# Samples' attention in two steps of four tiles instead of four of two, with a fifth place for cached tiles

## The chip, the core and the metric

The kernel runs on one core of a Trainium2 chip. A core has five engines with a queue of their own each, worked through in order: TensorE (PE in the profile; PEld is its weight load) for matrix products, VectorE (DVE), ScalarE (ACT), GpSimd (POOL) and SyncE (SP), which here issues transfers between the memory outside the core (HBM) and the on-chip memory SBUF. TensorE writes to PSUM, from where VectorE and ScalarE copy results. An engine that needs another's result waits at a semaphore, and all that stands behind that instruction in its queue waits too.

The metric is the device time of one execution in microseconds (us), lower is better. Three runs of the kernel before give 1091.49, 1091.80 and 1091.83 us, median 1091.8.

## The reference

One layer of a decoder for two groups that share all weights: a prompt of 512 tokens and 8 samples of 8 tokens. The layer has three blocks, each with a residual: a mixer (Mamba heads and mLSTM heads), an attention over a memory, and a feed-forward network. The change is in the second block. Cut to what matters:

```python
qx = (u @ w_xq).reshape(bsz, length, X_HEADS, X_HEAD_DIM)          # 4 heads of 256
sc = jnp.einsum('blhd,bmhd->bhlm', qx, mem_k) * (X_HEAD_DIM ** -0.5)
pr = jax.nn.softmax(sc, axis=-1)
o = jnp.einsum('bhlm,bmhd->blhd', pr, mem_v).reshape(bsz, length, X_WIDTH) @ w_xo
x = x + _rms(o) * g_post_x
```

For the prompt, keys and values of the memory (256 entries) are computed here from `w_mem_k` and `w_mem_v`. For the samples they come from a cache, `cache_mem_k` and `cache_mem_v`, with 256 entries and 4 heads of 256 for each of the 8 samples: 8 MB of keys and 8 MB of values in 32-bit floats, which are read once.

## The kernel before

Prompt and samples are 576 columns of the same matrices (512 and 64), so that each weight is loaded once for both. Weights are multiplied in two parts: each 128x1024 tile of weights is loaded by SyncE into one of two buffers `raw` (line 175), ScalarE rounds it to `whi` (L180), VectorE and POOL subtract for the rest `wlo` (L187), and TensorE takes three products, whi with the high part of the activations (L202), whi with their low part (L203), wlo with the high part (L205). There are three buffers of `whi` and `wlo`, so a cast waits until TensorE is through with the tile three before, and a load waits until the split of the tile two before is done.

The attention runs over the four heads of the prompt from 3 down to 0. For each head TensorE computes the queries (`xq`, tiles ps_xq), the memory's keys (`mem_key`, ps_mk, 48 products), the previous head's outputs (`attn_values`: transposes ps_pt at L1367, products ps_ov at L1374 to L1376), the scores (`attn_scores`, ps_at, L1344 to L1346), and the memory's values (`mem_value`, ps_v, L795 to L797).

The samples' attention is work in between, written as Python generators. `attn_samples_k(hb)` computes scores and softmax for four samples and all heads, `attn_samples_v(hb)` the outputs; there are two halves `hb` of the samples, so four generators. Each calls `pick`, which goes over four samples in two pairs. For each sample `pick` loads two tiles of the cache (512 KB each, `cached`, L1388, issued by SyncE), and for each tile takes four products, one for each head, of 32 columns of weights (the queries or probabilities, 128x32) with 256 columns of the tile, in full 32-bit floats (L1401). The four heads' products write to four different groups of 32 output partitions. A pair's two samples share one PSUM tile (ps_sa for keys, ps_os for values); VectorE then picks the right rows of it with a mask (L1409, L1411). After the second pair come the softmax (VectorE, ScalarE) and two transposes (ps_pts at L1427), or the transposes of the output (ps_ots at L1436).

`pick` gives control back (`yield`) after the first sample of each pair and after the first pair: four steps of two tiles, eight products each, per generator. The steps are spread by hand over the program: `sample_step(m)` advances the generator, placed after instruction `m`. In the loop over heads there are four such places: after the first `xq`, in `mem_key` after the first half, in `attn_scores` after the first scores, and after `mem_value`. So one generator runs in each of the heads 2, 1 and 0. The fourth one, `attn_samples_v(0)`, runs in the following loop, the output projection `xo` (tiles ps_xo, 24 products of 288 columns for each j): after j = 0, 1, 3 and 5.

The cached tiles rotate over a list `kv` of four places: three in the tile `s5` (named kva in the profile) and one of its own (kvb). A load into a place waits until TensorE has read the tile that was there.

The order of the instructions on each engine in this part is not written out by hand: a scheduler, which plays the program through with its own estimates of times, places them within the constraints that `issue_after` sets. It may cut a step into pieces or join two. A transfer is placed in SyncE's queue by the same scheduler.

Of the kernel before, what the change touches and what calls it, by code (L numbers as in the profile page):

```python
# [11 lines left out]
F32 = mybir.dt.float32  # L12
# [7 lines left out]
P = 128  # L20
# [95 lines left out]
def build(nc, tc, ctx, I, O):  # L116
# [14 lines left out]
    def SL(slot, name, dt=F32, shape=(P, KT, T)):  # L131

        return big.tile(list(shape), dt, name=name, tag="s%d" % slot, bufs=1)
# [5 lines left out]
    def MP(name="m"):  # L139
        return pa.tile([P, 512], F32, name=name, tag="a")  # L140
# [14 lines left out]
    def C32(k):  # L155
        a, b = _c32[k]
        return c32[:, a:b] if b <= NLONG else c32e[:, a - NLONG:b - NLONG]
# [50 lines left out]
    def gemm2(units, xh, xl, evac, name, halves=(0, 1), alloc=None, order=None, parts=HALVES):  # L208
        for i in halves:
            t0, n = parts[i]  # L210
            ps = (alloc or GP)(name)[:, :n]
            m = gemm(ps, units, xh, xl, t0, n, order=order)
            evac(t0, n, ps)
        return m

    def act(t):
        return lambda k, t0, n: t[:, k, t0:t0 + n]
# [492 lines left out]
    for g in range(2):  # L710
# [13 lines left out]
        for h in range(8):  # L724
            k, j = h % 2, (8 * g + h) // 2
# [421 lines left out]
    def weights(key, src, n=1024, pool=None, cut=CUT, acc=False):  # L1147

        for kept in recent.values():
            for k, w in kept:  # L1150
                if k == key:
                    return w
        kept = recent.setdefault(pool, [])
        kept.append((key, split_w(src, n, cut, acc, pool)))
        if len(kept) > (NWX if pool else 3):
            kept.pop(0)
        return kept[-1][1]

    st = ExitStack()
    at = st.enter_context(tc.tile_pool(name="attn", bufs=1, reuse_waits="tile"))  # L1160
# [60 lines left out]
    def out2(j, i):  # L1221
        return gemm2([(*weights(("o", j), I["wout"][j, 1], cut=1024), KT)], act(mixm_h), act(mixm_l), o2_evac(j), "ps_o2", [i])
# [30 lines left out]
    m = out2(7, 0)  # L1253
    with tc.issue_after(m.ins):
        rc = rstd_cols([ssq], HCHUNKS[1], "po1", alloc=B0)
    m = out2(6, 0)
# [9 lines left out]
    s5 = SL(5, "kva", F32, (P, 4608))  # L1266
# [3 lines left out]
    def sample_step(m):  # L1270

        with tc.issue_after(m.ins):
            next(steps, None)
# [4 lines left out]
    def mem_key(h, ws=None):  # L1278

        mk = at.tile([P, 2, 2, 256], F32R, name="mk", tag="mk", bufs=1)  # L1280
        mo = at.tile([P, 2, 256], F32, name="mko", tag="mo", bufs=2)
        for kk in range(2):
            ps = GP("ps_mk")[:, 0:256]
            m = gemm(ps, [(*(ws[kk] if ws else split_w(I["wmk"][2 * h + kk])), KT)], mem_act(0), mem_act(1), 0, 256)
            if kk == 0:
                sample_step(m)
            V.tensor_tensor(mo[:, kk, :], ps, rmem_b, op=ALU.mult)
            split(mk[:, 0, kk, :], mk[:, 1, kk, :], mo[:, kk, :], None if ws else G)
        S.dma_start(O["mk"][:, 2 * h:2 * h + 2, :], mo)
        return (mk, m) if ws else mk  # L1290
# [20 lines left out]
    def xq(j, i):  # L1311
        return gemm2([(*weights(("xq", j), I["wxq"][j], cut=1024 if i else CUT), KT)], act(u2h), act(u2l), q_evac(j), "ps_xq", [i])

    def q_evac(j):
        def ev(t0, n, ps):
            c = slice(t0, t0 + 256)
            A.copy(qh[:, j, c], ps[:, 0:256])
            V.tensor_tensor(ql[:, j, c], ps[:, 0:256], qh[:, j, c].bitcast(F32), op=ALU.subtract)
            if t0:
                A.copy(qsm[:, j, :], ps[:, 256:320])  # L1320
        return ev
# [10 lines left out]
    def attn_scores(h, mk):  # L1332
        pr = at.tile([P, 4, 256], F32, name="pr", tag="pr", bufs=1)
        mx = at.tile([P, 4], F32, name="mx", tag="mx", bufs=2)
        sm = at.tile([P, 4], F32, name="sm", tag="sm", bufs=2)
        for tp in range(2):
            pss = MP("ps_at")
            for t2 in range(2):
                t = 2 * tp + t2
                o = pss[:, t2 * 256:(t2 + 1) * 256]  # L1340
                for kk in range(2):
                    j = 2 * h + kk
                    a_, b_ = qh[:, j, t * P:(t + 1) * P], ql[:, j, t * P:(t + 1) * P]
                    mm(o, a_, mk[:, 0, kk, :], start=kk == 0, stop=False, skip_group_check=True)  # L1344
                    mm(o, b_, mk[:, 0, kk, :], start=False, stop=False, skip_group_check=True)
                    m = mm(o, a_, mk[:, 1, kk, :], start=False, stop=kk == 1, skip_group_check=True)  # L1346
            if tp == 0:
                sample_step(m)
            V.reduce_max(mx[:, 2 * tp:2 * tp + 2], pss.rearrange("p (a m) -> p a m", a=2), axis=AX.X)
            V.tensor_tensor(mx[:, 2 * tp:2 * tp + 2], mx[:, 2 * tp:2 * tp + 2], nscol[:, 2 * tp:2 * tp + 2], op=ALU.mult)  # L1350
            for t2 in range(2):
                t = 2 * tp + t2
                A.activation(pr[:, t, :], pss[:, t2 * 256:(t2 + 1) * 256], AF.Exp, scale=scol[:, t:t + 1],
                             bias=mx[:, t:t + 1], accum_out=sm[:, t:t + 1])
            c2 = slice(2 * tp, 2 * tp + 2)
            V.reciprocal(sm[:, c2], sm[:, c2])
            (V if tp else G).tensor_tensor(pr[:, c2], pr[:, c2], sm[:, c2].unsqueeze(2).to_broadcast([P, 2, 256]),
                                           op=ALU.mult)
        return pr
# [19 lines left out]

    kxs = ExitStack()  # L1380
    kx = kxs.enter_context(tc.tile_pool(name="kx", bufs=1, side="right", reuse_waits="tile"))
    kv = [s5[:, 1024 * i:1024 * i + 1024] for i in range(3)] + [kx.tile([P, 1024], F32, name="kvb")]
    turn = [0]

    def cached(src):
        t_ = kv[turn[0] % len(kv)].rearrange("p (h m) -> p h m", h=4)
        turn[0] += 1
        S.dma_start(t_, src)  # L1388
        return t_

    def pick(dst, hb, src, lhs, name):

        for pair in range(2):
            ps = (B0, B1)[pair](name)
            for b2 in range(2):
                b = 2 * pair + b2
                o = ps[:, 256 * b2:256 * b2 + 256]
                for d in range(2):
                    t_ = cached(src[4 * hb + b, :, d])
                    for h in range(4):  # L1400
                        mm(o[32 * h:32 * h + 32, :], lhs(h, d), t_[:, h, :], start=d == 0, stop=d == 1,  # L1401
                           skip_group_check=True)
                if not b2:
                    yield
            for b2 in range(2):
                b = 2 * pair + b2
                o = ps[:, 256 * b2:256 * b2 + 256]
                if b == 0:
                    V.tensor_scalar(dst, o, C32("bmask")[:, 0:1], None, op0=ALU.mult)  # L1409
                else:  # L1410
                    V.scalar_tensor_tensor(dst, o, C32("bmask")[:, b:b + 1], dst, op0=ALU.mult, op1=ALU.add)  # L1411
            if not pair:
                yield
# [29 lines left out]
    mk, m = mem_key(3, wm[:2])  # L1443
    with tc.issue_after(m.ins):
        rc = rstd_cols([ssq], HCHUNKS[0], "po0", alloc=B0)
    mv, m = mem_value(3, wm[2:])
# [10 lines left out]
    m = xq(4, 1)  # L1457
    with tc.issue_after(m.ins):
        rc2[1] = rstd_cols([ssq2], HCHUNKS[1], "p21", alloc=B1)
    m = xq(5, 1)  # L1460
    with tc.issue_after(m.ins):
        rstd_rows(rc2[1][:, 2:3], HCHUNKS[1][2:], rb2, B1)
    m = xq(6, 1)
# [6 lines left out]
    last = None  # L1470
    for h in range(3, -1, -1):

        sample_step(xq(2 * h + 1, 0))
        xq(2 * h, 0)
        if last:
            mk = mem_key(h)
            attn_values(*last)
        pr = attn_scores(h, mk)
        if last:
            mv, m = mem_value(h)  # L1480
            sample_step(m)
        last = h, pr, mv
        steps = attn_samples_k(h - 2) if h > 1 else attn_samples_v(h)
    attn_values(*last)
    st.close()


    bx = ctx.enter_context(tc.tile_pool(name="bx", bufs=1, reuse_waits="tile"))
# [31 lines left out]
    for j in range(8):  # L1520
        step = xo(j, 0, wx if 3 < j < 7 else None)
        if j < 3:

            step(0, KT - 2)
            with tc.issue_after(ends[-1].ins) if j else ExitStack():
                ends.append(step(KT - 2, KT)[0])
        else:
            ends.append(step(0, KT)[0])

        if j < 2:  # L1530
            next(steps, None)
        elif j in (3, 5):
            sample_step(ends[-1])
    kxs.close()
    u3l = SL(5, "u3l", F32R)
# [502 lines left out]
    with tc.manual_schedule(engines={TE.engine, A.engine, V.engine, G.engine, S.engine}):  # L2038
# [9 lines left out]
        tp = tps.enter_context(tc.tile_pool(name="sums", bufs=1, side="right", reuse_waits="tile"))  # L2048
# [308 lines left out]
```

## Time and profile before

| What | Value |
|---|---|
| Median of 3 runs | 1091.8 us |
| Time of the profiled execution | 1092.94 us |
| Its span, from the first to the last instruction | 1091.2 us |
| TensorE busy | 1079.0 us (99% of the span) |
| VectorE, ScalarE, POOL busy | 753.5, 611.5, 225.2 us |
| Bytes moved by transfers | 182.29 MB, mean 167 GB/s |
| Mean granted clock of TensorE | 0.998 |
| First and last product of the samples' attention (L1401) | 543.8 and 658.7 us |
| Loads of cached tiles | 32 of 512 KB, from 360.0 us on (kvb) and 522.3 us on (kva) |

How to read it: the profile is one execution. A row of a timeline has the start in us from the span's start, the duration, the engine, the line, the operation, output and inputs, and how many instructions were merged. A row of the chain, which follows the work that ended last back from the end, has start, duration, engine, tile and line, with the count of merged records behind it. A row of a waits view has who waited for whom, the total in us, the number of times and the longest. A row of a windows view has the stretch, its length, then the busy time and count of PE, PEld, DVE, ACT and POOL, the granted clock, the busy share of the 16 DMA engines and GB/s. Each 32-bit product of L1401 is recorded as two matmuls, so eight products show as 16 records. Matmuls overlap, so the distance from start to start, not the duration of one, tells what one costs.

### The profile page before, as it was taken

To read this page: it belongs to the slowest core of one execution; us is meant where nothing else is said; L and a number is where in the kernel's file an instruction comes from. 1 tells how busy PE (TensorE), PEld (TensorE's weight loads), DVE (VectorE), ACT (ScalarE), POOL (GpSimd) and SP (SyncE) were. 2 spreads that over 40 slices of the span, in tenths; PEclk is the share of its full clock that TensorE was granted. 3 is DMA by queue.
4 is the path that set the end of the run, shared out by engine and by line. 5 is a ranking of instruction groups with operands and counts; after the bars stand their busy time and mean duration, and the time that the engine had idled before them with its cause. 6 is when DMAs were issued, how large, how long until landed. Compare 5 with 4: busy or idle time off the path is not lost.

```text
span 1091.2 us, 20715 instructions
## 1 busy us (share of the span) xinstructions
PE 1079.0 (99%) x8124; PEld 1021.6 (94%) x8124; DVE 753.5 (69%) x1507; ACT 611.5 (56%) x1098; POOL 225.2 (21%) x305
## 2 busy tenths in 40 slices
PE   9999999999999999999999999999999999999997
PEld 8999887778999999999988879999999999999997
DVE  6896785758877775569644546666567887787555
ACT  7867632355654555566544545646567566656653
POOL 1332643313213111000244301100011121111000
PEclk9999999999999999999999999999999999999999
DMA  6785634435655348653468765644486687577532
GB/s 206 176 160 127 163 110 172 164 91 172 191 149 154 102 148 287 202 201 114 143 216 278 274 232 175 224 150 100 118 182 146 149 203 170 115 190 183 128 130 88
DMA packets 58966, 182.29 MB, mean 167 GB/s; under 512 B 6604, under 2 KB 11852, under 8 KB 58356
## 3 DMA queue, kind: packets, MB, share of 16 engines
q1 hardware_dynamic: 42740, 138.06, 38.7%
q0 software_dynamic: 15552, 41.95, 19.7%
q8 instruction: 64, 1.05, 0.4%
q10 hardware_dynamic: 576, 0.95, 0.3%
q14 instruction: 34, 0.28, 0.1%
HBM read 160.28 MB, written 20.65 MB: 166 GB/s over the span
## 4 chain that ended last, share of the span: by engine, by line
PE 80%; DVE 6%; DMA 5%; ACT 5%; issue 3%; POOL 1%; SPq 0%; DVEq 0%; ACTq 0%; POOLq 0%
PE ps_in L203 4%; PE ps_in L202 4%; PE ps_in L205 4%; PE ps_v L815 3%; PE ps_g L1849 3%; PE ps_g L1850 3%; PE ps_u L1850 3%; PE ps_u L1851 3%; PE ps_g L1851 3%; PE ps_u L1849 3%; PE ps_dn L1849 2%; PE ps_dn L1850 2%; PE ps_dn L202 2%; PE ps_dn L203 2%; PE ps_dn L1851 2%
## 5 line engine op out<-in xcount | busy, mean ns | idle before, releaser
L202 PE MATMUL ps_in<-uh,whi 128*128 128x320 f32 (+1 forms) x544 | 162.9, 300 | 0.8 <-DVE cb L451 0.5
L205 PE MATMUL ps_in<-uh,wlo 128*128 128x320 f32 (+1 forms) x544 | 162.1, 298 | 0.3 <-DMA wlo<-win 0.3
L203 PE MATMUL ps_in<-ul,whi 128*128 128x320 f32 (+1 forms) x544 | 161.7, 297 | 0.0
L180 ACT CAST whi<-raw 128x1024 fp32r<-128x1024 f32 (+1 forms) x104 | 105.3, 1013 | 97.6 <-PE ps_in L203 25.8
L187 DVE TENSOR_TENSOR wlo<-raw,whi 128x512 fp32r<-128x512 f32 (+1 forms) x96 | 97.2, 1015 | 69.2 <-ACT whi L180 68.3
L202 PEld LDWEIGHTS ps_in<-uh,whi 128*128 128x128 f32 x544 | 102.7, 189 | 3.9 <-issue 1.7
L205 PEld LDWEIGHTS ps_in<-uh,wlo 128*128 128x128 f32 x544 | 102.2, 188 | 1.4 <-DMA wlo<-win 0.5
L203 PEld LDWEIGHTS ps_in<-ul,whi 128*128 128x128 f32 x544 | 102.3, 188 | 0.6
L185 POOL DMA_DIRECT2D wlo<-win x32 | 27.8, 869 | 80.4 <-ACT wlo L184 72.3
L1850 PE MATMUL ps_g<-b,whi 128*128 128x288 f32 x144 | 42.5, 295 | 0.0
L1850 PE MATMUL ps_u<-b,whi 128*128 128x288 f32 x144 | 42.4, 295 | 0.0
L1849 PE MATMUL ps_g<-b,whi 128*128 128x288 f32 x144 | 42.4, 294 | 0.0
L1849 PE MATMUL ps_u<-b,whi 128*128 128x288 f32 x144 | 42.2, 294 | 0.0
L1822 ACT CAST whi<-rawx 128x1024 fp32r<-128x1024 f32 (+1 forms) x26 | 25.6, 985 | 27.2 <-PE ps_dn L1850 13.7
L192 DVE TENSOR_TENSOR wlo<-sw,whi 128x1024 fp32r<-128x1024 f32 (+1 forms) x26 | 29.6, 1140 | 15.7 <-ACT whi L191 15.6
L202 PE MATMUL ps_xo<-qh,whi 128*128 128x288 f32 x128 | 38.7, 304 | 0.2 <-ACT whi L180 0.2
L205 PE MATMUL ps_o<-mixm_h,wlo 128*128 128x256 f32 (+1 forms) x128 | 38.0, 297 | 0.6 <-DVE wlo L187 0.6
L205 PE MATMUL ps_o<-mixs_h,wlo 128*128 128x320 f32 (+1 forms) x128 | 37.7, 295 | 0.0
L203 PE MATMUL ps_xo<-ql,whi 128*128 128x288 f32 x128 | 37.7, 296 | 0.0
L203 PE MATMUL ps_o<-mixs_l,whi 128*128 128x320 f32 (+1 forms) x128 | 37.7, 294 | 0.0
L202 PE MATMUL ps_xq<-u2h,whi 128*128 128x320 f32 (+1 forms) x128 | 37.7, 298 | 0.0
L203 PE MATMUL ps_o<-mixm_l,whi 128*128 128x256 f32 (+1 forms) x128 | 37.7, 294 | 0.0
(765 smaller groups left out, 3836.0 us busy)
## 6 DMA issues: line engine op xcount, KB each, us to landing
raw<-win SPq DMA_DIRECT2D x35, 512.0 KB, 4.0
raw<-wout SPq DMA_DIRECT2D x17, 512.0 KB, 3.6
raw<-wxq SPq DMA_DIRECT2D x13, 512.0 KB, 3.6
raw<-wgate SPq DMA_DIRECT2D x13, 512.0 KB, 3.6
raw<-wup SPq DMA_DIRECT2D x13, 512.0 KB, 5.0
wlo<-win POOLq DMA_DIRECT2D x24, 256.0 KB, 5.0
kva<-kc SPq DMA_DIRECT2D x12, 512.0 KB, 5.7
kva<-vc SPq DMA_DIRECT2D x12, 512.0 KB, 5.7
```

What stands on the lines that cost most here:

```text
L180: casts.append(A.copy(hi[:, :n], raw[:, :n]))
L185: G.dma_start(lo[:, a:b], src[:, a:b], accum_op=ALU.add)
L187: e.tensor_tensor(lo[:, a:b], raw[:, a:b], hi[:, a:b].bitcast(F32), op=ALU.subtract)
L192: (eng or V).tensor_tensor(lo, src, hi.bitcast(F32), op=ALU.subtract)
L202: mm(ps, wh, ah, start=i == 0, stop=False)
L203: mm(ps, wh, al, start=False, stop=False)
L205: m = mm(ps, tiles[order[c]][1], xh(order[c], t0, n), start=False, stop=c == len(tiles) - 1)
L815: mm(ps, a, b, skip_group_check=True, **kw)
L1822: A.copy(s.h3[:, s.all], s.r2[:, s.all])
L1849: mm(ps, wh, b[0][k], start=start and k == 0, stop=False, skip_group_check=True)
L1850: mm(ps, wh, b[1][k], start=False, stop=False, skip_group_check=True)
L1851: m = mm(ps, wl, b[0][k], start=False, stop=k == nk - 1, skip_group_check=True)
```

## The change

Three things. In `pick` the `yield` after the first sample of each pair is taken out, so that a generator has two steps of four tiles and sixteen products instead of four of two and eight. In the loop over heads the places after `xq` and in `attn_scores` go, those in `mem_key` and after `mem_value` stay; in the loop over `xo` the two steps come after j = 1 and j = 4 instead of after 0, 1, 3 and 5. And the list of places gets a fifth one, `kvc`, from the pool `at` of the attention's tiles. It is taken off the list when that pool is closed, before the loop over `xo`, so that the last generator rotates over four places again.

```diff
@@ attn_scores
-            if tp == 0:
-                sample_step(m)
@@
-    kv = [s5[:, 1024 * i:1024 * i + 1024] for i in range(3)] + [kx.tile([P, 1024], F32, name="kvb")]
+    kv = [s5[:, 1024 * i:1024 * i + 1024] for i in range(3)] + [kx.tile([P, 1024], F32, name="kvb"), at.tile([P, 1024], F32, name="kvc")]
@@ pick
                     for h in range(4):
                         mm(o[32 * h:32 * h + 32, :], lhs(h, d), t_[:, h, :], start=d == 0, stop=d == 1,
                            skip_group_check=True)
-                if not b2:
-                    yield
@@ loop over heads
-        sample_step(xq(2 * h + 1, 0))
+        xq(2 * h + 1, 0)
         xq(2 * h, 0)
@@
     attn_values(*last)
     st.close()
+    kv.pop()
@@ loop over xo
-        if j < 2:
+        if j == 1:
             next(steps, None)
-        elif j in (3, 5):
+        elif j == 4:
             sample_step(ends[-1])
```

No product, no transfer and no other operation is added or left out. In the built program the first load into the fifth place stands on SyncE among the loads of the memory (`memraw`, L1198) and of the mixer's output weights, which the profile before has at 401 to 405 us; the other engines have the same instructions as before, in another order between the first score and the middle of `xo`, and slightly so around the memory's loads.

## Prediction

> **What bounds the kernel now.** I read the page first, then its chain, then TensorE's waits, the chain in order of time and the timeline around the samples' attention (SyncE and ScalarE where a transfer matters).
>
> ```profile
> span 1091.2 us, 20715 instructions
> PE 1079.0 (99%) x8124; PEld 1021.6 (94%) x8124; DVE 753.5 (69%) x1507; ACT 611.5 (56%) x1098; POOL 225.2 (21%) x305
> PE 80%; DVE 6%; DMA 5%; ACT 5%; issue 3%; POOL 1%; SPq 0%; DVEq 0%; ACTq 0%; POOLq 0%
> ```
> ```profile
> 545.00:665.00 120.00, 119.61 (x1023) 104.40 (x1023) 61.51 (x114) 56.90 (x115) 33.63 (x25) 1.00 0.71 241
> ```
> ```profile
> PE ps_xo L202 <- ACT whi L180: 0.2, 1, 0.2
> PE ps_v L797 <- POOL wlo L187: 0.2, 1, 0.2
> ```
>
> TensorE is the bound. The second fence is the stretch that the change touches: TensorE busy 119.61 of 120 us, its clock full, DMA at 0.71, vector engines about half busy. From 500 to 720 us TensorE waits twice, 0.2 us each, both times for weights; it never waits for a cached tile. So time can come only from making TensorE's own stream shorter, or go by new waits. Busy hides one thing: how closely matmuls follow each other. The timeline at one sample step:
>
> ```profile
> 553.98 0.28 PE L205 MATMUL ps_mk<-memhl,wlo 128*128 128x256 f32 x1
> 554.19 0.64 PE L1401 MATMUL ps_sa<-kva,qsm 128*32 128x256 f32 x8
> 554.64 0.61 PE L1401 MATMUL ps_sa<-kvb,qsm 128*32 128x256 f32 x8
> 555.19 0.39 PE L202 MATMUL ps_mk<-memhl,whi 128*128 128x256 f32 x1
> 555.41 0.28 PE L203 MATMUL ps_mk<-memhl,whi 128*128 128x256 f32 x1
> 555.53 0.28 PE L205 MATMUL ps_mk<-memhl,wlo 128*128 128x256 f32 x1
> ```
>
> Ordinary products start 0.12 us apart (555.41, 555.53). A sample step has eight 32-column products, recorded as 16. From 553.98 to 555.41 is 1.43 us; less two ordinary products (0.24) the group costs 1.20, of which a part is the way in and out: 0.21 before the group and 0.22 behind it, where 0.12 is usual. The chain in order of time prices groups of other sizes:
>
> ```profile
> 543.85 0.99 PE ps_sa L1401 x12
> 544.83 0.43 PE ps_at L1344 x2
> 547.85 0.56 PE ps_sa L1401 x4
> 548.41 0.32 PE ps_xq L202
> 554.26 1.00 PE ps_sa L1401 x16
> 611.12 1.86 PE ps_os L1401 x32
> 612.98 0.32 PE ps_mk L205
> 631.61 0.98 PE ps_os L1401 x10
> 632.59 0.48 PE ps_pt L1367 x3
> 633.06 0.22 PE ps_ots L1436 x2
> 633.39 0.56 PE ps_os L1401 x6
> 633.95 0.33 PE ps_xo L202
> 634.28 0.44 PE ps_pt L1367 x4
> 637.01 0.57 PE ps_os L1401 x8
> 641.96 0.56 PE ps_os L1401 x6
> 658.08 1.00 PE ps_os L1401 x16
> ```
>
> Price = group plus the longer first product after it, less that product's usual 0.12 (0.13 at 288 columns). Eight products (first 554.26, last 658.08, eleven of them): 1.20. Sixteen (611.12): 1.86 + 0.32 - 0.12 = 2.06. Six (543.85): 0.99 + 0.43 - 0.24 = 1.18. Two (547.85): 0.76. So 0.34 us of a group is fixed (2 x 1.20 - 2.06), and a split step costs nearly two: six and two products 1.94 where eight cost 1.20.
>
> **The change, part by part.**
>
> *Fewer, longer groups.* The same 128 products are issued, in eight steps instead of sixteen. Where they fall is in the order of the built programs, since a scheduler sets it. Before: eleven groups of eight (13.2), one of sixteen (2.06), six and two (1.94), a mixed run at 631.61 with transposes in it (0.98 + 0.48 + 0.22 + 0.56 + 0.33 - 0.13 = 2.44), four transposes alone at 634.28 (0.44 + about 0.11 = 0.55), and pieces of four, one and three at 637 to 642 (0.77 + 0.75 + 0.76 = 2.28): 22.5 us. After: seven groups of sixteen (14.4), the step that the scheduler still cuts into four, one, three and eight (2.28 + 1.20), and two runs of four transposes (1.10) and one of two (0.22), which now stand alone: 19.2 us. **Difference -3.3 us**, all of it on TensorE and so on the path; by single timeline gaps instead of the chain I get 3.2. As bounds, from the same rows: only eight fixed parts saved, 2.7; every piece at its dearest, 3.6. I take 3.2.
>
> The Trainium skill, "TensorEngine Tiling (Array Packing)", Key Properties, says that changing the tiling mode drains TensorE; "TensorE: Matmul & The Clock Gate", Single matmul latency, puts the drain at about 175 ns. By these alone 19 groups becoming 11 would save 8 x 2 x 0.175 = 2.8 us, an estimate from those pages, and transposes would cost no switch. The fixed 0.34 above is twice 0.17, so the trace agrees on the switch; it adds the short groups' poor overlap.
>
> *Two waits on weights.* The 0.2 at ps_v L797 ends a chain of transfer, cast and subtraction:
>
> ```profile
> 572.60 0.33 SPq L175 DMA_DIRECT2D raw<-wmk  x1
> 581.26 0.33 SPq L175 DMA_DIRECT2D raw<-wmv  x1
> 586.96 1.05 ACT L180 CAST whi<-raw 128x1024 fp32r<-128x1024 f32 x1 [2.92 <-PE ps_pt L1367]
> 588.08 3.50 POOL L187 TENSOR_TENSOR wlo<-raw,whi 128x512 fp32r<-128x512 f32 x2 [2.98 <-ACT whi L180]
> ```
>
> The transfer at 572.60 must land before that at 581.26 may go. In the new order the first is queued ahead of the cached tiles and its predecessor's cast ahead of ScalarE's exponentials, about 1 us sooner by the built order, while TensorE's own work between is about 0.5 us longer (two sixteens, 4.1, for three eights, 3.6). So the wait should go: 0 to -0.2, I take 0. Late next would be ps_xo L202, which waits for evacuations that are not changed.
>
> *Four tiles a step, five places.* Each place is filled again once its product has read it. Before, two of a step's two tiles are loaded a whole step ahead; after, one of four is, and three load between steps.
>
> ```profile
> DMA to landing us min/median/max: 4.0/5.7/6.8
> DMA to landing us min/median/max: 3.7/6.5/8.1
> ```
>
> (First line kva, second kvb.) Steps start 10.7 us apart or more: the closest in the loop have 72 products of 0.12 (8.6) behind a group of 2.06, and the third reload goes 1.5 after the start. Cover 9 us or more against 6.8, 8.1 at worst: 0. If it were gone, each us of lateness costs 1 us. On SyncE a reload that waits for its reader holds the weight load queued behind it (wxq behind the first step, wxo behind the cut one); a group reads a tile every 0.5 us, so a load is held 2 us at most, in a stretch where TensorE's waits for weights sum to 0.4: 0. POOL does the same operations in a slightly other order, busy 33.63 of 120 us: 0.
>
> *Behind the loop four places for a step of four*, so none is ahead. This is the tightest place; before, two tiles were loaded there:
>
> ```profile
> 628.01 1.00 PE ps_os L1401 x16
> 648.94 0.80 PE ps_xo L205 x6
> ```
>
> In the new order the group of sixteen (1.9), 36 products of ps_xo at 0.13 (4.8) and the three transpose runs (1.3) stand before the first new tile's products: about 8.3 us from the group's start. Its load goes 0.6 after the start (one tile's products), so 7.7 us of cover; the second tile, behind the o_mv store, goes at 1.5 and is wanted at 9.5: 8.0; the last two are wanted near 14, behind the ps_ov products. At the median 0, at 8.1 us 0.4. I take 0, and keep 0.4.
>
> ```profile
> 628.00:632.00 4.00, 4.00 (x44) 3.06 (x44) 2.85 (x8) 3.09 (x8) 1.04 (x1) 1.00 0.78 244
> 636.00:640.00 4.00, 4.00 (x28) 2.67 (x27) 0.45 (x1) 0.00 (x0) 0.00 (x0) 1.00 1.04 415
> ```
>
> Weights, four tiles and the store are 2.9 MB: 7 us at the 415 GB/s of the second row, 11.8 at the 244 of the first. At the worse rate, served in the order of issue, the first tile still lands about 5 and the second about 8 us after the group's start.
>
> *The fifth tile's first load* moves to about 402 us, on SyncE between loads of the memory and of wout. 0.52 MB at 400 GB/s is 1.3 us of transfer that the wout weights may be late by.
>
> ```profile
> 406.00:411.00 5.00, 5.00 (x40) 5.00 (x39) 2.25 (x5) 3.09 (x7) 0.00 (x0) 1.00 1.00 400
> PE ps_o L205 <- DVE wlo L187: 0.6, 1, 0.6
> ```
>
> DMA is full there, but the second row is TensorE's only wait between 395 and 475: 0, and 1.3 if that cover were gone.
>
> *ScalarE's order.* The second wmk cast now stands before an evacuation of ps_xq and the samples' exponential, and waits for a load; behind them wait TensorE's two ps_pts transposes. These come after 68 products and a group (10 us), the cast about 7 us after the group's start: 0, up to 1 if the load takes 8.1.
>
> **Sum:** -3.2 against the profiled execution: span 1091.2 to 1088.0, its time 1092.9 to 1089.7. The runs' median 1091.8 lies 1.1 below that execution, so the median should be **1088.6 us**. A measurement here can tell about 0.2% (2.2 us) from no change.
>
> **Rivals.**
> A, slower: a step of four waits for its tiles. Place: the seven steps behind the first. For: one or none of four is loaded ahead, and slices reach 100% DMA. Against: covers of 7.7 to 9 us against landings of at most 8.1. It decides from landings of about 10 us on: seven waits of 0.8 us (5.6) make 1088.6 + 5.6 = 1094.2.
> B, about the same: the weights pace the loop, and TensorE only waits longer at wlo and whi. For: the 586.96 chain was just in time. Against: the rows give TensorE more work between, not less, and its waits sum to 0.4 of 120 us. If two of the 3.2 us are so given back: 1090.6.
> C: the change doesn't do what it says, the longer groups costing as much per product as short ones. Only the row at 611.12 speaks for the price of sixteen, but it is this very operation: 1091.8.
>
> **Chances.** Forecast 0.66, A 0.14, B 0.15, C 0.05. A half-strong A ends near no change, and a weak B is still faster by 0.2%: faster 0.67, same 0.20, slower 0.13. The range reaches down to the dearest price with both weight waits gone (3.6 + 0.4, and 0.2 for the measurement): 1087.6; up past B to a weak A, 1091.5. The forecast's own range is 1087.8 to 1089.6.
>
> **What would show it.** Right: the chain of the changed kernel has rows of x32 for the samples near 1.86, eight such or seven and pieces; the span between the first sample product and the end of ps_xo is some 3 us shorter; TensorE's waits from 500 to 720 stay under 0.5 us and name no cached tile; the time before 540 us is unchanged. Wrong: a wait of TensorE at ps_sa or ps_os on a transfer of kva, kvb or kvc (A), above all the first step behind the loop; longer waits on whi or wlo (B); x32 rows near 2.1 (C); a new wait at ps_o near 410 to 470 (the early load).

## The result and the profile after

The changed kernel takes 1087.57 us (median of 6 runs, 1086.96 to 1088.87) against 1091.82 us (6 runs, 1091.49 to 1092.46): ratio 0.9961, 95% interval 0.9948 to 0.9974. That is 4.25 us less, where 3.2 were forecast; the time lies 0.03 us under the lower end of the range. These 0.03 are far less than runs of one kernel scatter (five later runs of the changed kernel have the median 1087.84), so it is the stretches below that tell how far the forecast was off, and where.

First the head of the page of the changed kernel: span, busy times and the chain's shares.

```profile
span 1085.2 us, 20708 instructions
...
PE 1075.0 (99%) x8124; PEld 1022.1 (94%) x8124; DVE 752.4 (69%) x1507; ACT 610.9 (56%) x1098; POOL 228.0 (21%) x305
...
PE 86%; DVE 5%; ACT 4%; issue 2%; DMA 2%; POOL 0%; DVEq 0%; SPq 0%; ACTq 0%; POOLq 0%
```

The span is 6.0 us shorter, more than the runs' medians differ. To see which part belongs to the change, I cut each trace at three landmarks: the first product of ps_o, of ps_xq and of ps_g (the first of the feed-forward network). The change's steps lie between ps_xq and ps_g. The last column ends with TensorE's last product; 7.0 us of other engines' work follow it in both kernels. These are starts read from the timelines, in us, the traces of further runs with them:

| Trace | start to ps_o | ps_o to ps_xq | ps_xq to ps_g | ps_g to the end of the last product |
|---|---|---|---|---|
| before | 389.70 | 115.62 | 187.94 | 390.88 |
| before, three more | 390.59, 389.42, 389.06 | 116.21, 114.56, 116.90 | 187.84, 187.79, 187.84 | 390.86, 390.88, 390.84 |
| changed | 389.01 | 114.56 | 183.75 | 390.88 |
| changed, two more | 391.16, 390.96 | 114.56, 114.56 | 183.74, 183.74 | 390.85, 390.87 |

The third column repeats within 0.15 us: the change is worth **4.1 us there** (187.85 in the mean of four, less 183.74), and nothing behind it. The first two columns vary by up to 2.3 us from execution to execution of the same kernel. Of the 6.0 us between the two spans, 1.8 is such chance (0.7 ahead of ps_o, 1.06 in a wait at ps_o that two other traces of before have and one has not). The medians' 4.25 agree with the 4.1.

Windows of that stretch, before and then after (columns as before):

```profile
505.32:693.26 187.94, 187.55 (x1529) 171.32 (x1529) 109.89 (x229) 95.69 (x198) 46.53 (x40) 1.00 0.64 215
```
```profile
503.57:687.32 183.75, 183.53 (x1529) 170.91 (x1529) 109.26 (x230) 95.06 (x198) 48.20 (x40) 1.00 0.64 217
```

Same instructions, same clock, nearly the same transfers: TensorE's stream itself is shorter. TensorE's waits of the changed kernel from 500 to 720 us are one line, and the chain in order of time shows the sample groups (start, duration, tile, line, records):

```profile
PE ps_xo L202 <- ACT whi L180: 0.2, 1, 0.2
```
```profile
550.42 1.86 PE ps_sa L1399 x32
552.28 0.32 PE ps_mk L202
...
567.42 1.86 PE ps_sa L1399 x32
...
577.90 1.86 PE ps_sa L1399 x32
...
594.80 1.86 PE ps_sa L1399 x32
...
607.63 1.86 PE ps_os L1399 x32
...
622.27 1.86 PE ps_os L1399 x32
...
626.31 0.44 PE ps_pt L1365 x4
...
630.21 0.57 PE ps_os L1399 x8
...
631.38 0.55 PE ps_os L1399 x2
...
632.36 0.56 PE ps_os L1399 x6
...
636.05 1.00 PE ps_os L1399 x16
...
648.08 1.86 PE ps_os L1399 x32
```

Seven groups of sixteen products at 1.86, and one step in pieces of four, one, three and eight, as the built order said. No cached tile is waited for, and the wait at ps_v is gone. That wait, in the timeline of the kernel before:

```profile
588.67 0.28 PE L796 MATMUL ps_v<-whi,memhl 128*128 128x256 f32 x1
588.79 0.38 PE L797 MATMUL ps_v<-wlo,memhl 128*128 128x256 f32 x1
589.01 0.28 PE L795 MATMUL ps_v<-whi,memhl 128*128 128x256 f32 x1
...
589.47 0.28 PE L796 MATMUL ps_v<-whi,memhl 128*128 128x256 f32 x1
589.93 0.38 PE L797 MATMUL ps_v<-wlo,memhl 128*128 128x256 f32 x1 [0.18 <-POOL wlo L187]
590.15 0.28 PE L795 MATMUL ps_v<-whi,memhl 128*128 128x256 f32 x1
```

Its note says 0.18. By starts it cost more: 589.47 to 589.93 is 0.46 where 0.12 is usual, 0.34 lost, and the steps at 588.79 and 589.93 are 0.22 each, 0.10 lost twice. Together 0.5 us. In the other three traces of before the same place loses 0.4, of which at most 0.14 is recorded as idle.

So the 4.1 us are: groups (with the transposes among and behind them) 25.9 to 22.5 by starts, -3.4; the wait at ps_v, -0.5 in this trace and -0.4 in the other three; 0.2 to 0.3 that I could not place (0.1 of it slightly closer products of ps_mk).

### The profile page after: what moved, and what is told of

Read it like the earlier page. It is cut to its first block, busy times and chain, and to the rows that moved or that the text cites. A ratio compares the mean times of both kernels' runs of the same rounds, so it can differ in the third digit from the quotient of the medians.

```text
span 1085.2 us, 20708 instructions
## 1 busy us (share of the span) xinstructions
PE 1075.0 (99%) x8124; PEld 1022.1 (94%) x8124; DVE 752.4 (69%) x1507; ACT 610.9 (56%) x1098; POOL 228.0 (21%) x305
## 3 DMA queue, kind: packets, MB, share of 16 engines
q8 instruction: 64, 1.05, 0.4%
## 4 chain that ended last, share of the span: by engine, by line
PE 86%; DVE 5%; ACT 4%; issue 2%; DMA 2%; POOL 0%; DVEq 0%; SPq 0%; ACTq 0%; POOLq 0%
PE ps_in L203 4%; PE ps_in L202 4%; PE ps_in L205 4%; PE ps_v L815 3%; PE ps_o L205 3%; PE ps_o L203 3%; PE ps_g L1846 3%; PE ps_g L1847 3%; PE ps_o L202 3%; PE ps_u L1847 3%; PE ps_u L1848 3%; PE ps_u L1846 3%; PE ps_g L1848 3%; PE ps_dn L1846 2%; PE ps_dn L1847 2%
## 5 line engine op out<-in xcount | busy, mean ns | idle before, releaser
L180 ACT CAST whi<-raw 128x1024 fp32r<-128x1024 f32 (+1 forms) x104 | 105.2, 1013 | 100.0 <-PE ps_in L203 25.9
L187 DVE TENSOR_TENSOR wlo<-raw,whi 128x512 fp32r<-128x512 f32 (+1 forms) x96 | 93.7, 978 | 75.1 <-ACT whi L180 74.0
L1798 ACT CAST whi<-raw 128x1024 fp32r<-128x1024 f32 (+1 forms) x26 | 25.6, 983 | 21.8 <-PE ps_g L1847 9.7
```

The costliest lines, as they stand in the source:

```text
L180: casts.append(A.copy(hi[:, :n], raw[:, :n]))
L187: e.tensor_tensor(lo[:, a:b], raw[:, a:b], hi[:, a:b].bitcast(F32), op=ALU.subtract)
L1798: s.c1 = A.copy(s.h1[:, s.all], s.r1[:, s.all])
```

## The experiments

Two theories of the groups stood against each other, and against the idea that the tiles' fifth place and the order of transfers bring the gain. *Quarters*: the products of a step run on four groups of 32 output columns side by side, and a group costs 0.34 us fixed plus 0.43 for each product of its fullest quarter (16: 0.34 + 4 x 0.43 = 2.06; 8: 1.20; pieces of one, three or four alike 0.77). *Products*: 0.34 plus 0.1075 for each product. The prediction's rows of sixteen and eight can't tell these apart; its rows of six and two (1.18 and 0.76, where *products* gives 0.99 and 0.56) speak for the quarters. All stretches below are from ps_xq to ps_g in that run's trace: before 187.85, changed 183.74.

**Parts of the change alone.** First, only the loop over heads is joined; the last generator yields after each sample as before, with its four places behind the loop over heads.

```diff
-def pick(dst, hb, src, lhs, name):
+def pick(dst, hb, src, lhs, name, small=False):
...
+                if small and not b2:
+                    yield
...
-        if j == 1:
+        if j < 2:
             next(steps, None)
-        elif j == 4:
+        elif j in (3, 5):
```

> Steps joined in the loop over heads only; behind the loop four steps of two tiles, as before. Group theory (a group costs 0.34 us and 0.43 us for each product of its fullest column quarter): in the loop 14.8 us of groups become 12.4, -2.4; the wait on the weights of ps_v goes too, -0.5; together 1088.6 to 1088.9. Rival, transfers (the gain comes from the tiles' fifth place and the order of the loads, which this kernel keeps): 1087.6, as the whole change. Rival, the gain lies behind the loop: 1091 or more.

Measured 1089.24 us (8 runs; ratio 0.9974, 0.9964 to 0.9984), stretch 184.79 (-3.06), groups 23.6 (-2.3), no wait at ps_v. The reverse, joined steps only in the last generator:

```diff
-        xq(2 * h + 1, 0)
+        sample_step(xq(2 * h + 1, 0))
...
+            if tp == 0:
+                sample_step(m)
...
+                if small and not b2:   # small for all generators but the last
+                    yield
```

> Steps joined behind the loop only; in the loop sixteen-product steps stay split in two. Group theory: behind the loop the pieces cost 6.7 us before and here, by the built order (12, 2, 2 and 16 products), 1.63 + 0.77 + 0.77 + 2.06 = 5.2, so -1.4, and the wait at ps_v stays: 1090.4. Rival, transfers: 1087.6. Rival, the gain lies in the loop: 1091.8.

Measured 1090.83 us (11 runs; 0.9988, 0.9979 to 0.9997), stretch 186.08 (-1.77), groups 24.4 (-1.5). Both halves come out near what the groups' prices say, in the groups of the trace and in time (each time is 0.3 to 0.4 above its expectation, beside runs of the kernel before with the median 1092.16 instead of 1091.8); the fifth place is in both kernels and does not bring the whole gain in either. In the second one the wait at ps_v is gone although the loop's groups are those of before, so it can go without the longer groups; what sets it was not isolated (the place alone, below, does not remove it).

**The places alone.** The change with four places, then the kernel before with five.

```diff
-    kv = [...] + [kx.tile([P, 1024], F32, name="kvb"), at.tile([P, 1024], F32, name="kvc")]
+    kv = [...] + [kx.tile([P, 1024], F32, name="kvb")]
...
-    kv.pop()
```

> The whole change without the fifth place. Group theory: the same groups in nearly the same order; the reload of a tile has some 10 us from its reader to its next use against landings of at most 8.1, so nothing is lost: 1087.6. Rival, the fifth place carries part of the gain (a tile ahead, its first load at 402 us ahead of the weights of ps_o): each of the seven steps waits 0.3 to 0.8 us for a tile, 1089.5 to 1093.

Measured 1089.09 us (9 runs; 0.9973, 0.9963 to 0.9983), 1.5 more than the changed kernel's first median. Two traces: stretch 185.54, and in the second

> The change without the fifth place, a second trace. If the lacking place sets the stretch from ps_o to ps_xq: 115.6 again; by chance 114.6 as likely. From ps_xq to ps_g 185.5 again, with a wait at the first step behind the loop for a cached tile, if that wait belongs to the four places; 183.7 if it was chance.

184.12 (that execution took 1088.44 us; ps_o to ps_xq 114.56). TensorE's waits of the first, from 500 to 700 us:

```profile
PE ps_os L1399 <- DMA kva<-vc: 0.9, 2, 0.7
PE ps_pts L1423 <- DVE kva L1420: 0.6, 1, 0.6
PE ps_xo L202 <- ACT whi L180: 0.2, 1, 0.2
```

With joined steps and four places a cached tile is late at the first step behind the loop, in both traces (0.9 and 0.4), and once the samples' softmax is late too. The expectation of no loss was wrong: here the fifth place is worth 0.4 to 1.8 us. It is so only together with the long steps, for the place alone, with the short steps of before,

```diff
+    kv = [...] + [kx.tile([P, 1024], F32, name="kvb"), at.tile([P, 1024], F32, name="kvc")]
...
+    kv.pop()
```

> The kernel before with the fifth place and nothing else. Group theory: the groups are those of before, so 1091.8. Rival, the place alone gives part of the gain (the first load of the fifth tile stands elsewhere, the wait at ps_o goes): 1090 to 1091.

gave 1092.72 us (11 runs; ratio 1.0005, 0.9996 to 1.0014) and a stretch of 188.49, 0.6 more than before: the same groups, and two waits at ps_v on wlo (0.38 and 0.33 lost by starts) where before has one.

**The price of a group.** The second product of each pair left out for all heads, then left out for three of the four heads.

```diff
-                    for h in range(4):
+                    for h in range(0 if d else 4):       # half
+                    for h in range(1 if d else 4):       # one quarter
-                        mm(..., start=d == 0, stop=d == 1,
+                        mm(..., start=True, stop=True,                  # half
+                        mm(..., start=d == 0, stop=d == 1 or h > 0,     # one quarter
```

> The changed kernel, where the second product of a sample is kept for the first head alone and left out for the other three: ten products to a step, of which one column quarter still holds four and the others two. Theory of the quarters: a step costs 2.06 still, only the pieces get shorter, -0.9: 1086.7. Rival, what counts is the number of products (0.34 and 0.1075 for each): a step costs 1.42, -6: 1081.5.

The chain of that kernel, at its first step:

```profile
551.68 1.84 PE ps_sa L1399 x20
553.53 0.32 PE ps_mk L202
```

Twenty records, that is ten products, last 1.84 us where sixteen last 1.86. By starts the seven such groups cost 2.03 to 2.17. Six products fewer save nothing as long as one quarter still has four: the quarters' theory holds, and the products' theory (1.42) falls. This case's trace so agrees with the Trainium skill, "TensorEngine Tiling (Array Packing)", Key Properties, which says that different tiles of the array work in parallel. Whether it is the fullest quarter that counts or the number of rounds over the four heads, these runs can't tell: the products come in the order of the heads, and both numbers are the same in every group. The stretch is 182.85, -0.9 as expected. The time is 1089.16 (8 runs; 0.9971, 0.9961 to 0.9981) and not 1086.7. In the profiled execution ps_g to the end of the last product takes 393.24 instead of 390.9, with a wait of 1.2 us at ps_dn (the feed-forward network's last product, with the weights wdown). The instructions of all engines and the transfers stand in the changed kernel's order there; ahead of that wait ScalarE's cast waits 2.66 us for a tile of wdown, where the changed kernel's trace has 1.05. Why that transfer landed later, and whether it did so in the other seven runs, is open.

> The changed kernel with only the first of each two products of a sample (the second half of every sum is left out, its tiles are still loaded): eight products to a step where sixteen were. Theory of the quarters (a group costs 0.34 us fixed and 0.43 for each product of its fullest column quarter): 2.06 becomes 1.20 seven times, the pieces 3.7 become 1.5; -8.2, so 1079.4. Rival, a group costs mostly its fixed part: above 1083.

The groups came out as expected (1.19 to 1.21 each) and the time did not: 1087.57 us (4 runs; 0.9956, 0.9939 to 0.9973), stretch 183.84. Eight us of products were taken away and nothing was gained. TensorE's waits from 500 to 700 us, and two windows:

```profile
PE ps_os L1399 <- DMA kva<-vc: 3.8, 1, 3.8
PE ps_v L795 <- ACT whi L180: 1.1, 1, 1.1
PE ps_xo L202 <- ACT whi L180: 0.2, 1, 0.2
PE ps_v L797 <- DVE wlo L187: 0.2, 1, 0.2
```
```profile
628.00:632.00 4.00, 0.22 (x6) 0.08 (x8) 1.50 (x3) 2.29 (x4) 0.00 (x0) 1.00 0.90 354
632.00:635.00 3.00, 3.00 (x17) 2.24 (x18) 1.25 (x3) 0.00 (x0) 0.00 (x0) 0.51 0.65 220
```

With TensorE's work shortened, transfers set the pace: the first step behind the loop waits 3.8 us for a cached tile (transfers at 0.90 of their time in that window), and then the granted clock is 0.51. The prediction's rival A (tiles late) and rival B (weights pace the loop) are both real in this stretch; they begin some us of TensorE work away.

**The cut step held together.** The changed kernel's one step in pieces costs 0.76 + 0.84 + 0.88 + 1.20. Put behind a product that the scheduler may not pass, it stands whole:

```diff
         if j == 1:
-            next(steps, None)
+            sample_step(ends[-1])
```

> The whole change, with the first step behind the loop put behind the last product of xo(1), so that its sixteen products stand in one group. Group theory: the four pieces (0.76 + 0.84 + 0.88 + 1.20 = 3.7) become 2.06, -1.6 against the changed kernel: 1086.0; the 0.4 at ps_xo may go as well: 1085.6. Rival, tiles late: the next step now comes about 9 us behind this one with four places, so a wait at ps_os on a cached tile takes the gain: 1087 to 1089. Rival, pieces cost no more than whole groups: 1087.6.

It got slower: 1091.03 us (11 runs; 0.9988, 0.9978 to 0.9998), stretch 188.50. The groups are whole (2.06), but now TensorE waits for weights of xo. Waits, timeline and windows of that kernel:

```profile
PE ps_xo L202 <- ACT whi L180: 2.6, 2, 1.8
```
```profile
648.77 0.64 PE L1399 MATMUL ps_os<-kvb,kva 128*32 128x256 f32 x8
651.25 0.40 PE L202 MATMUL ps_xo<-qh,whi 128*128 128x288 f32 x1 [1.84 <-ACT whi L180]
651.49 0.29 PE L203 MATMUL ps_xo<-ql,whi 128*128 128x288 f32 x1
652.53 0.61 PE L202 MATMUL ps_xo<-qh,whi 128*128 128x288 f32 x1 [0.75 <-ACT whi L180]
652.94 0.45 PE L203 MATMUL ps_xo<-ql,whi 128*128 128x288 f32 x1
653.18 0.45 PE L205 MATMUL ps_xo<-qh,wlo 128*128 128x288 f32 x1
653.42 0.45 PE L202 MATMUL ps_xo<-qh,whi 128*128 128x288 f32 x1
```
```profile
652.00:655.00 3.00, 2.47 (x10) 2.47 (x11) 2.43 (x4) 0.48 (x1) 0.00 (x0) 0.50 0.50 124
655.00:658.00 3.00, 3.00 (x15) 3.00 (x14) 0.74 (x1) 1.05 (x1) 0.00 (x0) 0.50 0.69 229
```

Two things. The weights: a place is filled again only when its products have run. In the changed kernel the first piece runs at 630.2, and SyncE issues the next step's loads from 630.84 on; here the step runs at 638.2 and they go from 638.86 on, all four ahead of the wxo weights. SyncE's queue in the changed kernel, then here:

```profile
630.84 6.16 SPq L1386 DMA_DIRECT2D kva<-vc  x3
637.11 1.35 SPq L1386 DMA_DIRECT2D kvb<-vc  x1
...
642.68 6.18 SPq L175 DMA_DIRECT2D raw<-wxo  x3
```
```profile
638.86 1.93 SPq L1386 DMA_DIRECT2D kva<-vc  x3
640.89 0.37 SPq L1386 DMA_DIRECT2D kvb<-vc  x1
641.31 11.56 SPq L175 DMA_DIRECT2D raw<-wxo  x3
```

And the clock: behind the wait the products follow at 0.24 us, not 0.13, with a granted clock of 0.50 from about 651.9 to 658.7. A wait of 2.6 us cost some 3 us more behind it.

Whether the loads do it was tried by leaving the last four out of this same kernel:

```diff
-        S.dma_start(t_, src)
+        if turn[0] < 29:
+            S.dma_start(t_, src)
```

> The kernel with the whole step held behind xo(1), without the last four loads of cached tiles: the last step multiplies what already lies in the places. Left out: these loads, so the last two samples' values are wrong tiles. Theory of the collision (there the four loads go out together 8 us later than in the changed kernel, the weights of xo are queued behind them, TensorE waits 2.6 us at ps_xo and its clock then stands at half for some 6 us): without the loads the weights land in 4 us, no wait, no slow stretch: 1085.6 to 1086.0. Rival, the order of casts or of products makes the wait, not the loads: 1090 to 1091.

1086.95 us (5 runs; 0.9955, 0.9942 to 0.9967), stretch 183.42: 5.1 us less than with the loads, no wait on whi and no slow clock in this stretch. TensorE's waits from 500 to 720 us:

```profile
PE ps_os L1400 <- ACT kva L1425: 0.7, 1, 0.7
PE ps_xo L203 <- DVE ql L192: 0.2, 1, 0.2
```

The collision of loads is shown. The time misses the 1086.0 by one us; the profiled execution has a wait of 0.7 at the first step of values (on ScalarE's copy of the transposed probabilities) and two at ps_xo on ql, the low part of its activations (0.25 and 0.42 lost by starts).

Later places for both steps, which then both stand whole:

```diff
-        if j == 1:
-            next(steps, None)
-        elif j == 4:
+        if j in (2, 5):
             sample_step(ends[-1])
```

> The whole change, with the two steps behind the loop put behind xo(2) and xo(5) instead of xo(1) and xo(4); both stand whole. Group theory: as with the step held together at xo(1), 1086.0, with some 11 us between the two steps. Rival, later is too late: the samples' transposes come later and the second half of xo waits for their evacuation: above 1087.

1092.5 us (11 runs; 1.0001, 0.9992 to 1.001), stretch 187.68, again through ps_xo on weights (2.1 and 0.8 us) with the clock at half behind it from about 652.4 to 655.8. The reason named in the expectation, that the transposes come too late, is not what the trace shows.

Earlier instead: behind the first part of xo(2).

```diff
-            step(0, KT - 2)
+            m = step(0, KT - 2)
+            if j == 2:
+                sample_step(m)
...
-        if j == 1:
-            next(steps, None)
-        elif j == 4:
+        if j == 4:
```

> The whole change, with the first step behind the loop put behind the first part of xo(2), so about 3 us ahead of the held-together step and 2 to 5 us behind where the changed kernel begins it; built as thirteen, one ordinary product, three. Group theory: 2.06 + 0.77 where four pieces cost 3.7, -0.9, and the loads go out about 5 us later than in the changed kernel: 1086.7 if the weights still come in time. Theory of the collision: TensorE waits at ps_xo for weights by 0 to 1 us, 1086.7 to 1088.5, and if the clock falls with it 1089 to 1090.

1086.93 us (5 runs; 0.9955, 0.9943 to 0.9968), stretch 183.05, 0.7 less than the changed kernel; its groups cost 21.8 (thirteen at 2.13, three at 0.86). No new wait. Held whole there, with the last parts of xo(0) to xo(2) behind the step:

```diff
+            held.append(step)
             if j == 2:
+                with tc.issue_after(m.ins):
+                    m = next(steps)
+                for step in held:
+                    with tc.issue_after(m.ins):
+                        m = step(KT - 2, KT)[0]
+                        ends.append(m)
```

> As the kernel with the step behind the first part of xo(2), with the last parts of xo(0) to xo(2) held behind the step, so that its sixteen products stand whole. Theory of the quarters: 2.06 where thirteen and three cost 2.13 + 0.86, so 0.9 less than that kernel's 1086.9: 1086.0. Theory of the collision, if it decides here: the loads of the next step go out when the step is over, no later than there, so no new wait; if there is one at ps_xo all the same, 1086.5 to 1087.5.

1088.13 us (5 runs; 0.9963, 0.995 to 0.9977), stretch 183.64: the group is whole at 2.06, and the 0.9 us are given back at ps_xo on wlo (0.8) and at the next step (2.32). So again weights, not products. The early place and the changed kernel were then timed side by side:

> The changed kernel on the chip of the next run, for a comparison of the two: 1087.6 by its first time, with 183.7 us from ps_xq to ps_g (-4.1 against before: groups -3.4, the wait at ps_v -0.5, the rest -0.2).

> The step behind the first part of xo(2) once more, beside the changed kernel. Theory of the quarters: its groups are 0.7 us shorter (21.8 against 22.5), its stretch from ps_xq to ps_g 183.05 again, its time 0.7 below the changed kernel's. Rival, the difference of the first times (1086.93 against 1087.57) was chance: no difference.

Changed kernel 1087.84 us (5 runs; 0.9964, 0.995 to 0.9978), early place 1087.62 us (5 runs; 0.9957, 0.9945 to 0.997). The stretches repeat, 183.74 and 183.04; the medians differ by 0.2, less than the runs scatter. The early place is better by 0.7 us in both its traces, and by an amount that the runs can't confirm in the whole time.

**The wait at ps_o.** Three more traces of the kernel before and one of the changed kernel asked whether the 1.06 us between ps_o and ps_xq belong to the fifth tile's early load.

> The kernel before once more, for its trace. From the start of ps_o to the start of ps_xq it took 115.62 us, the changed kernel 114.56. If the fifth place's early load sets that: 115.6 again, with a wait at ps_o on wlo. If it is chance of the execution: 114.6 is as likely. From ps_xq to ps_g 187.9, whatever the other is.

> The changed kernel once more, for its trace. If the fifth place's early load sets the stretch from ps_o to ps_xq: 114.6 again; if it is chance: 115.6 is as likely. From ps_xq to ps_g 183.7, 4.2 less than before.

> The kernel before, a third trace. If the stretch from ps_o to ps_xq is 1.0 us longer because the fifth place is lacking: 115.6 to 116.2 and a wait at ps_o on wlo, as in both traces so far. If it is chance of the execution: 114.6 is as likely.

> The kernel before, a fourth trace, for the same question: 115.6 to 116.2 if the lacking fifth place sets it, 114.6 as likely if chance does.

Before: 116.21, 114.56, 116.90 (times 1094.31, 1091.47, 1093.52). Changed: 114.56 (1089.1). So the kernel before can do without that wait. Among the six traces without the fifth place four have 1.0 to 2.3 us there; among fourteen with it one has 1.0 and one 0.2. The wait may be rarer with the fifth place; but the kernel before with the place added was not faster in its median (1092.72), so this stays open and I count nothing for it.

## Why the prediction was right and where it was not

*Fewer, longer groups* (forecast -3.3, taken as -3.2): right in kind and size, -3.4. The joint group costs 2.06, as the one row of sixteen had said, the transposes alone cost 0.44 rather than 0.55, the short pieces of one and three 0.84 and 0.88 rather than 0.75. "A split step costs nearly two" was right for a reason that the prediction did not see: pieces cost by their fullest quarter, so four and one product cost the same.

*Two waits on weights* (taken as 0, bounds 0 to -0.2): **this is the term that failed.** The prediction expected the wait at ps_v to go, but set it at nothing, and bounded its worth by the 0.2 that the waits view records. It went and was worth 0.4 to 0.5: the 0.18 recorded as idle was 0.34 from start to start, and the products behind the two on wlo (588.79 and 589.93) each came 0.10 late as well. The reason given for its going, weights that come sooner, fits the traces: "about 1 us sooner by the built order" was 4.4 us there (the last load of wmv ahead of that wait goes out 75.9 us after the start of ps_xq before, 71.6 after). That it is the cause was not shown; with joined steps behind the loop alone the wait goes with a load only 0.4 us sooner. With -3.4, -0.4 to -0.5 and 0.2 to 0.3 unplaced the sum is -4.1 instead of -3.2; with the first two alone the median would have been forecast at 1087.9 to 1088.0. The wait at ps_xo stayed, as expected.

*Four tiles, five places* (0): right, no cached tile is waited for in three traces. *Behind the loop* (0, kept 0.4): right, and the tightest place was named rightly: with four places throughout, or with shorter groups ahead of it, it is this first step that waits, by 0.4, 0.9 and 3.8 us.

*The fifth tile's first load* (0) and *ScalarE's order* (0): nothing in the traces of the changed kernel speaks against them. "The time before 540 us is unchanged" can't be read from one pair of traces, in which chance made 1.8 us.

*The sum against the profiled execution* (span to 1088.0): it was 1085.2, 1.8 of the difference by chance. Taking the median 1.1 us below that execution was sound: it has 1.06 us of wait at ps_o, which another execution of the same kernel (1091.47 us) does without.

*Rivals.* A did not occur, but its price was set wrong: "each us of lateness costs 1 us" fails for the waits of two to four us here, behind which the clock was halved. B did not occur: the weights came sooner, not later, and the same weights undo the gain as soon as the step moves (the step held whole, and the later one). C is excluded by the rows of 1.86.

## What to carry to other kernels

Price small products on quarters of the array by their fullest quarter and a fixed entry and exit (0.75 to 0.88, 1.20 and 2.06 us here for one to four, eight and sixteen), and price a wait by the gap between starts, not by its recorded idle. Where a product frees the place of the next transfer, its position also sets when that transfer starts: here pieces that cost 1.6 us of TensorE more than a whole step kept a collision of loads away that cost 5.1. Compare stretches between landmarks over several traces before a difference of one us between two spans is explained.

## What the hardware showed beyond what was expected

The clock can fall behind short waits. In three runs TensorE waited 1.84 and 0.75 us with two products between, 2.1 and 0.8 us, and 3.8 us; each time the granted clock then stood at 0.5, for 6.8, 3.4 and 3.4 us (worked out from the mean clock of windows of half a us to one us). The length of a wait alone does not decide it. The wait of 1.2 us at ps_dn in the kernel with ten products has no drop behind it, but in both further traces of the changed kernel a wait of 0.9 and 1.0 us at ps_ss (a sum of squares), near 24 us, with ten products of one column behind it, was followed by a clock of 0.50 for 3.4 us (from 26.8 and 26.6 us on). In six other traces the clock stood at 0.50 for 3.4 us from about 80 us on, with no recorded wait over 0.41 us shortly before. What decides stays open. It bears on the table at the start: wait and slow stretch put those two executions some 2.7 us further behind the first trace of the changed kernel, and 2 us of it are left at ps_o (391.16 and 390.96 against 389.01).

The Trainium skill, "TensorE: Matmul & The Clock Gate", Part 1, puts the half rate after at least one idle window of about 3.4 us, and the return after a busy window of the same length. The lengths here are about one and two such windows, so the trace agrees on the return; on the fall it does not, as only the wait of 3.8 us is that long, and two of the first three came with 2.6 and 2.9 us of recorded waiting and products in between.

Six of sixteen products could be left out of a group for 0.02 us, as long as one quarter stayed full.
